# Splitting the operands of a recurrent unit: an early part two units ahead, and token-pair products in 64x64 tiles

## The chip, the cores and the metric

The kernel runs on one core of a Trainium2 chip. A core has a matrix engine (TensorE, in the profile PE, with its weight loads listed apart as PEld), a vector engine (VectorE, DVE), a scalar engine (ScalarE, ACT), a general engine (GpSimd, POOL) and SyncE (SP), which here issues the DMAs. Each engine works through a queue of its own in order and waits on semaphores for the others. Operands lie in SBUF (128 partitions), products of TensorE land in PSUM, and transfers between SBUF and DRAM are DMAs. The metric is the device time of one execution in microseconds (us); less is better.

## The reference, cut to what matters

The program is a decoder trunk of two layers over 1024 tokens of width 1024. Layer 0 mixes tokens by attention, layer 1 by a recurrence (RWKV-7) over 12 heads of 64 channels; both have a feed-forward part. The change is in layer 1's recurrence alone:

```python
def step(S, inp):
    r_t, w_t, k_t, v_t, a_t, b_t = inp
    sa = jnp.einsum("bhij,bhj->bhi", S, a_t)
    S = S * w_t[:, :, None, :] + sa[..., None] * b_t[:, :, None, :] + v_t[..., None] * k_t[:, :, None, :]
    y = jnp.einsum("bhij,bhj->bhi", S, r_t)
    return S, y
```

It is called with `r, decay, k, v, -kk, kk * a`, where `kk` is the normalised key and `a` a gate. Each head has a 64x64 state S, which every token decays, corrects (`sa` by `b`) and adds to (`v` by `k`); `y` reads it out.

## The kernel before, in words

The recurrence is computed in chunks of CH = 64 tokens. Inside a chunk, the tokens' effect on each other is a 64x64 matrix of products of token pairs for each head; the corrections within a chunk need the inverse of a triangular 64x64 matrix made from one of these, called N. Between the chunks the state is carried on, one chunk after the other.

A *unit* n (0 to 11) is four heads (two *pairs*; a pair is two heads on the partition halves A = 0 to 63 and B = 64 to 127) and QT = 256 tokens, thus four chunks. Units 0 to 3 are the four quarters of the tokens of the first two pairs, 4 to 7 of the next two, and so on. The steps of a unit, with their lines:

- `prepare(n)` (from L947): allocates the unit's tiles, loads r, k, v and two gates from DRAM (L964, L967; pool `ld` with two buffers, of which one unit takes two), and normalises the keys (L973 to L992).
- `products(n)` (from L996) calls `unit` for each of two pairs. `unit` (from L1010) makes the running decay with a scan on DVE (L1017), exponentials on ACT (L1020, L1022), the tile AR (the corrected key and r, each decayed) and F, and with the inverse decay BKz, in which each head's rows are written for one head at a time and the other half is zero (L1035, L1037). On PE, BKz against AR in 128x128 tiles gives all token-pair products of one head and chunk (L1042): its rows hold, for one head, N and R in one half and the operands of the sequence in the other. DVE masks them into the tile ARK (L1043); ACT copies N and R out of ARK (L1044, L1045) and then writes AR over their place (L1046). PE transposes BKz (L1052, eight a pair), ACT takes half of it as `bkt` (L1053). `rkk` and `bv` (L1056 to L1059) are for the output. At the end v is transposed into W (L1004 to L1008). ARK has two buffers, used in turn: unit n+2 writes the one that unit n's sequence reads.
- `invert(n)` (from L1063): N goes to DRAM (L1070) and comes back as 16x16 blocks (`nb`, L1072); POOL inverts all blocks at once with 28 small operations that depend on each other (L1077, L1078); the blocks go to DRAM (L1081) and come back as X (L1084). Then two rounds for each pair merge 16x16 blocks to 32x32 and 64x64: a transpose on DVE (L1089), products on PE in 64x64 tiles (L1093, L1099), masking and adding on DVE (L1095, L1100).
- `sequence(n)` (from L1103): for each of four chunks in turn, products of ARK with W (L1124, L1140), a copy Rs (L1134), the product with X (L1146), a copy into W (L1150), the state for the next chunk (L1154, L1157), and the output's part with R (L1116); at the end `yd` is copied out (L1159).
- `finish(n)` (from L1162): normalises the output and stores it.

The order of the program is at L1192 to L1215. In turn n: `sequence(n)`, `invert(n+1)`, `prepare(n+2)`, `finish(n)`, `products(n+2)`. Between them stand *pieces* of other work, 88 in all (`fill`): the input projections of later heads (24 matrix products each, L149 to L151), memory attention, and first parts of the output projection (six matrix products each); 12 run before, seven by FILL[12], and FILL[n] in turn n. They are tied behind the first matmul of each chunk of the turn (`issue_after`). A planner decides each engine's order when the program is built, from its own estimates of time; what is written earlier goes first where both are ready, and on the chip each engine keeps that order. After turn 10, `fill(99)` and the loads for the rest of the output projection are written (L1211 to L1215), ahead of turn 11.

Of the kernel before, what the change touches and what calls it, by code (L numbers as in the profile page):

```python
# [10 lines left out]
F32 = mybir.dt.float32  # L11
# [18 lines left out]
FILL = (4, 4, 3, 4, 5, 3, 11, 9, 8, 9, 9, 0, 7)  # L30
# [36 lines left out]
class Trunk:  # L67
# [588 lines left out]
    def rwkv(self, rows_src):  # L656
# [8 lines left out]
        with ExitStack() as so:  # L665
# [240 lines left out]
            with ExitStack() as s:  # L906
# [33 lines left out]
                for t in XD:  # L940
                    nc.sync.dma_start(t.rearrange("a b -> (a b)").rearrange("(p f) -> p f", p=P), BKz.rearrange("p c h t -> p (c h t)")[:, 0 : PITCH // 16])
# [5 lines left out]
                def prepare(n):  # L947
# [5 lines left out]
                    d["N"], d["R"] = (up.tile([P, 2, NC, CH], F32, name=c) for c in "NR")  # L953
                    d["pC"] = up.tile([P, 2, NC], F32, name="pC", bufs=3)
                    d["bv"] = up.tile([P, 2, QT], F32, name="bv")
                    d["bkt"] = up.tile([P, 2, NC, P], F32, name="bkt")
                    d["W"] = W = up.tile([P, 2, NC, 2, CH], F32, name="W")
                    if q == 0:
                        nc.gpsimd.memset(W[A, :, 0, 0, :], 0.0)
                        nc.gpsimd.memset(W[B, :, 0, 1, :], 0.0)  # L960
# [35 lines left out]
                def products(n):  # L996
                    d = DU[n]
                    ld, W = d["ld"], d["W"]
                    for u in range(2):
                        unit(d, u, ld[u], d["sa"][u], d["kk"][u])  # L1000
# [9 lines left out]
                def unit(d, u, rkv, sga, kk):  # L1010
                    p = d["pa"] + u
                    r, k, v = (rkv[:, j, :] for j in range(3))
                    sg, at = sga[:, 0, :], sga[:, 1, :]
                    ark, Rm, Nm, bkz = d["ark"][:, u], d["R"][:, u], d["N"][:, u], BKz
# [19 lines left out]
                    bz = lambda hd: bkz[:, :, hd, :].rearrange("p c (h t) -> p c h t", h=2)  # L1034
                    nc.vector.tensor_mul(bz(0)[A], F[A], c3(pi)[A][:, :, None, :].broadcast_to([64, NC, 2, CH]))  # L1035
                    for j in range(2):
                        nc.vector.tensor_mul(bz(1)[B, :, j, :], F[B, :, 1 - j, :], c3(pi)[B])  # L1037

                    for R, hd in HD:
                        ga = psg.tile([P, NC, P], F32, name="ps_ga", tag="g")  # L1040
                        for c in range(NC):
                            nc.tensor.matmul(ga[:, c, :], bkz[:, c, hd, :], AR[:, c, :, :].rearrange("p h t -> p (h t)"), start=True, stop=True)  # L1042
                        nc.vector.tensor_mul(ark[:, :, hd, :], ga, MM[:, None, :].broadcast_to([P, NC, P]))  # L1043
                        nc.scalar.copy(Nm[R], ark[R, :, hd, 0:64])  # L1044
                        nc.scalar.copy(Rm[R], ark[R, :, hd, 64:P])  # L1045
                        nc.scalar.copy(ark[R, :, hd, :], AR[R].rearrange("p c h t -> p c (h t)"))  # L1046

                    for c2 in range(0, NC, 2):
                        pbk = psg.tile([P, 2, 4, CH], F32, name="ps_bk", tag="g")
                        for c in range(2):  # L1050
                            for hd in range(2):
                                nc.tensor.transpose(pbk[:, c, 2 * hd : 2 * hd + 2, :], bkz[:, c2 + c, hd, :], self.ident)  # L1052
                        nc.scalar.copy(d["bkt"][:, u, c2 : c2 + 2, :].rearrange("p c (h j) -> p c h j", h=2), pbk[:, :, 0:4:3, :])  # L1053

                    rkk = t1("rkk", tag="sq")
                    nc.vector.scalar_tensor_tensor(c3(rkk), c3(r), self.col("rk", p), F[:, :, 1, :], op0=ALU.mult, op1=ALU.mult)  # L1056
                    pbv = psx.tile([P, QT], F32, name="ps_bv", tag="x")
                    nc.tensor.matmul(pbv, blk, rkk, start=True, stop=True)
                    nc.vector.tensor_mul(d["bv"][:, u, :], pbv, v)  # L1059
# [3 lines left out]
                def invert(n):  # L1063
                    d = DU[n]
                    N = d["N"]
                    nd, xd = ND[n % 2], XD[n % 2]
                    nb = up.tile([64, 16, 16], F32, name="nb", bufs=1)
                    xb = up.tile([64, 16, 16], F32, name="xb", bufs=1)
                    for R, hd in HD:
                        nc.sync.dma_start(rows_of(nd, hd), N[R].rearrange("p u c t -> p (u c t)"))  # L1070
# [9 lines left out]
                    for h in range(8):  # L1080
                        nc.sync.dma_start(blocks_of(xd, h), xb[8 * h : 8 * h + 8])  # L1081
                    d["X"] = X = up.tile([P, 2, NC, CH], F32, name="X")
# [108 lines left out]

                N = 2 * NPAIR  # L1192
                prepare(0)
                products(0)
                invert(0)
                fill(FILL[12])
                prepare(1)
                products(1)
# [704 lines left out]
```

## Time and profile before

| | |
|---|---|
| median of 3 runs | 2689.64 us (2686.9 to 2694.15) |
| profiled execution | 2686.54 us, span 2684.7 us |
| mean granted TensorE clock in it | 0.974 |
| the recurrence's sequences | first ends at 1463.0, last at 1991.8 us |

The page of the profile gives the busy time of each engine; "busy time in stretches" gives, for each stretch of time, its length, then the busy time of PE, PEld, DVE, ACT and POOL with the number of instructions, the TensorE clock that was granted as a share of full speed, the share of DMA time, and GB/s. The timeline has the start, the duration, the engine, the line, and what is written from what; in brackets stands how long the engine sat idle before and what ended it. A row of the waits has the instruction that waited, whom it waited for, the total in us, how often, and the longest. A row of a group has the count, then busy time and mean ns of one, then idle time before it and what ended that. A row that gives "min/median/max" has durations in ns and the first and last start. An fp32 matmul shows as two instructions.

### The profile page before, as it was taken

What the parts mean: (1) busy time and instruction counts of PE and PEld (TensorE: products, weight loads), DVE (VectorE), ACT (ScalarE), POOL (GpSimd) and SP (SyncE); (2) the same over time, 40 slices, a digit from 0 to 9 for tenths busy, and PEclk for the clock granted to TensorE, in tenths of its full rate; (3) what the DMA queues carried; (4) which work ended last, traced back from release to release, by engine and by line L of the source; (5) the groups of instructions that cost most, each with busy time, mean ns of one, the idle gap of its engine ahead of it and who ended that gap; (6) DMA issues with size and microseconds to landing.
All of it is one profiled execution on the core that took longest, in us unless ns stands there. A gap on an engine that the chain in (4) does not pass through costs nothing. (4 is left out here: it accounts for less than half of the span.)

```text
span 2684.7 us, 41293 instructions
## 1 busy us (share of the span) xinstructions
PE 2543.4 (95%) x15901; PEld 2064.7 (77%) x15901; DVE 1795.9 (67%) x3283; ACT 1219.9 (45%) x2032; POOL 222.2 (8%) x525
## 2 busy tenths in 40 slices
PE   8999999999999999999989999889888999999998
PEld 7877776778888788887867777677666888878886
DVE  5567766577666687675246656887669656568677
ACT  4465555254444433348343433564216444443343
POOL 0012232000000000000011211222200000000000
PEclk9999999999999999999999999999889999999999
DMA  4100002334443867535632233324214444386761
GB/s 168 58 26 17 9 21 72 123 108 164 150 147 133 300 247 271 206 106 202 218 107 71 81 99 86 99 74 145 70 57 149 161 153 151 136 332 231 270 228 71
DMA packets 263828, 370.50 MB, mean 138 GB/s; under 512 B 41104, under 2 KB 139792, under 8 KB 263632
## 3 DMA queue, kind: packets, MB, share of 16 engines
q1 hardware_dynamic: 263488, 367.60, 40.1%
q8 instruction: 125, 2.05, 0.3%
q14 instruction: 71, 0.58, 0.1%
q10 hardware_dynamic: 144, 0.26, 0.0%
HBM read 258.75 MB, written 109.05 MB: 137 GB/s over the span
## 5 line engine op out<-in xcount | busy, mean ns | idle before, releaser
L143 ACT CAST Xh<-wraw 128x1024 fp32r<-128x1024 f32 (+1 forms) x138 | 139.8, 1039 | 216.4 <-PE ps_z L1623 75.7
L149 PE MATMUL ps_in<-Xh,whi 128*128 128x512 f32 x480 | 195.8, 410 | 14.5 <-ACT whi L143 8.8
L150 PE MATMUL ps_in<-Xl,whi 128*128 128x512 f32 x480 | 193.1, 402 | 0.5 <-DVE Xl L144 0.5
L151 PE MATMUL ps_in<-Xh,wlo 128*128 128x512 f32 x480 | 193.0, 403 | 0.0
L143 ACT CAST Xl<-wraw 128x1024 fp32r<-128x1024 f32 x103 | 105.2, 1051 | 150.5 <-PE ps_y L1623 48.4
L144 DVE TENSOR_TENSOR Xh<-wraw,Xh 128x1024 fp32r<-128x1024 f32 x115 | 138.0, 1220 | 48.4 <-ACT Xh L143 47.9
L144 DVE TENSOR_TENSOR wlo<-wraw,whi 128x1024 fp32r<-128x1024 f32 (+3 forms) x93 | 105.9, 1139 | 71.5 <-ACT whi L143 70.8
L144 DVE TENSOR_TENSOR Xl<-wraw,Xl 128x1024 fp32r<-128x1024 f32 x103 | 123.8, 1221 | 34.0 <-ACT Xl L143 33.5
L143 ACT CAST whi<-wraw 128x1024 fp32r<-128x1024 f32 (+3 forms) x93 | 88.3, 953 | 120.0 <-PE ps_in L150 51.2
L149 PEld LDWEIGHTS ps_in<-Xh,whi 128*128 128x128 f32 x480 | 92.7, 193 | 36.0 <-ACT whi L143 8.8
L1285 PE MATMUL ps_f<-Xh,N 128*128 128x512 f32 x320 | 106.7, 397 | 4.4 <-ACT N L143 2.7
L151 PEld LDWEIGHTS ps_in<-Xh,wlo 128*128 128x128 f32 x480 | 92.4, 193 | 19.9
L150 PEld LDWEIGHTS ps_in<-Xl,whi 128*128 128x128 f32 x480 | 92.7, 193 | 19.2 <-DVE Xl L144 1.0
L625 ACT ACTIVATE E<-ps_s,mx,SC 128x128 f32<-128x128 f32 (+7 forms) x96 | 79.5, 832 | 51.1 <-DVE mx L623 24.5
L628 POOL TENSOR_TENSOR E<-E,l 128x768 f32<-128x768 f32 (+5 forms) x60 | 83.8, 1401 | 201.6 <-DVE l L626 101.3
L1285 PE MATMUL ps_f<-TB,N 128*128 128x512 f32 x384 | 91.9, 389 | 0.7 <-ACT N L143 0.7
L1623 PE MATMUL ps_y<-Xh 128*128 128x512 f32 x384 | 90.1, 389 | 0.0
L1623 PE MATMUL ps_z<-Xh 128*128 128x512 f32 x384 | 89.6, 389 | 0.0
L1623 PE MATMUL ps_z<-Xl 128*128 128x512 f32 x384 | 89.6, 389 | 0.0
L1623 PE MATMUL ps_y<-Xh,Xh 128*128 128x512 f32 x360 | 85.0, 390 | 0.0
L1285 PEld LDWEIGHTS ps_f<-TB,N 128*128 128x128 f32 x384 | 72.0, 188 | 16.0 <-ACT N L143 1.1
L1623 PEld LDWEIGHTS ps_z<-Xl 128*128 128x128 f32 x384 | 72.1, 188 | 15.0
(519 smaller groups left out, 6611.3 us busy)
## 6 DMA issues: line engine op xcount, KB each, us to landing
wraw<-in_w_ff_dram SPq DMA_DIRECT2D x182, 512.0 KB
wraw<-h_d SPq DMA_DIRECT2D x108, 512.0 KB
h_d<-slot SPq DMA_DIRECT2D x128, 256.0 KB
h_d<-tr SPq DMA_DIRECT2D x64, 256.0 KB
wraw<-in_w_in_dram SPq DMA_DIRECT2D x31, 512.0 KB
lo_d<-l_st SPq DMA_DIRECT2D x36, 256.0 KB
rkv_d<-rkv_st SPq DMA_DIRECT2D x36, 256.0 KB
rkv<-rkv_d SPq DMA_DIRECT2D x24, 384.0 KB
```

The costliest lines, as they stand in the source:

```text
L143: h = self.nc.scalar.copy(hi, src)
L144: l = self.nc.vector.tensor_sub(lo, src, f32(hi))
L149: mm(ps, wh, xh, start=first, stop=False)
L150: mm(ps, wh, xl, start=False, stop=False)
L151: mm(ps, wl, xh, start=False, stop=last)
L625: nc.scalar.activation(E3[:, g, :], S[:, g * w0 : g * w0 + n], AF.Exp, bias=mx[:, g : g + 1], scale=SC[:, i : i + 1], accum_out=l[:, g : g ...
L628: nc.gpsimd.tensor_mul(E3, E3, l[:, :, None].broadcast_to([P, nh, n]))
L1285: yield nc.tensor.matmul(ps, A[x][:, k, :], B[y][:, k, :], start=fresh and k == 0 and i == 0, stop=k == 3 and i == 2, skip_group_check=True)
L1623: m = nc.tensor.matmul(ps[t], A[x][:, u, t * P : (t + 1) * P], B[y][:, u, :], start=fresh and i == u == j == 0, stop=end and i == last_ an ...
```

## The change

- `prepare(n)` no longer allocates N, R, bv, bkt and W. N and R become one tile NR, with three buffers.
- `early(n)` is new: for both pairs `decays` (the first part of the old `unit`: scan, exponentials, AR, F, and BK, now one dense tile without zeros), then the products of each head's own rows with its own columns in 64x64 tiles, masked by DVE straight from PSUM into NR; then `substitute(n)`, the DRAM trips and POOL's chain up to the store of the blocks.
- `late(n)` is new: the other products of token pairs, in 64x64 tiles from the rows of one half to the partitions of the other half, masked into ARK; the copies of AR into ARK; four transposes a pair and not eight; bv, and v into W.
- `merge(n)` is the rest of `invert(n)`, from the load of X on.
- The order in turn n is `sequence(n)`, `merge(n+1)`, `prepare(n+2)`, `early(n+2)`, `finish(n)`, `late(n+2)`. FILL is new, with seven pieces in turn 11, and `fill(99)` with the last loads is written after the last turn.

The core of the diff:

```diff
-FILL = (4, 4, 3, 4, 5, 3, 11, 9, 8, 9, 9, 0, 7)
+FILL = (4, 3, 4, 3, 4, 3, 11, 9, 7, 7, 7, 7, 7)
...
-                BKz = kp.tile([P, NC, 2, P], F32, name="BKz")
-                for t in [cmp_, BKz]:
-                    nc.gpsimd.memset(t, 0.0)
+                nc.gpsimd.memset(cmp_, 0.0)
+                nc.gpsimd.memset(ARK[0], 0.0)
...
-                    d["N"], d["R"] = (up.tile([P, 2, NC, CH], F32, name=c) for c in "NR")
+                    d["NR"] = up.tile([P, 2, NC, 2 * CH], F32, name="NR", bufs=3)
...
+                def early(n):
+                    d = DU[n]
                     for u in range(2):
-                        unit(d, u, ld[u], d["sa"][u], d["kk"][u])
+                        decays(d, u, d["ld"][u], d["sa"][u], d["kk"][u])
+                    substitute(n)
...
+                def late(n):
...
+                    for u in range(2):
+                        ark, AR, BK = d["ark"][:, u], d["AR"][u], d["BK"][u]
+                        ga = psg.tile([P, NC, P], F32, name="ps_ga", tag="g")
+                        for c in range(NC):
+                            for R, hd in HD:
+                                nc.tensor.matmul(ga[HD[1 - hd][0], c, :], BK[R, c, 1, :], AR[R, c, :, :].rearrange("p h t -> p (h t)"), start=True, stop=True)
+                        for R, hd in HD:
+                            O = HD[1 - hd][0]
+                            nc.scalar.copy(ark[R, :, hd, :], AR[R].rearrange("p c h t -> p c (h t)"))
+                            nc.vector.tensor_mul(ark[O, :, hd, :], ga[O], MM[O, None, :].broadcast_to([64, NC, P]))
+
+                        pbk = psg.tile([P, NC, P], F32, name="ps_bk", tag="g")
+                        for c in range(NC):
+                            nc.tensor.transpose(pbk[:, c, :], BK[:, c, :, :].rearrange("p h t -> p (h t)"), self.ident)
+                        nc.scalar.copy(d["bkt"][:, u, :, 0:64], pbk[:, :, 0:64])
+                        for R, hd in HD:
+                            nc.scalar.copy(d["bkt"][R, u, :, 64:P], pbk[HD[1 - hd][0], :, 64:P])
...
-                    AR = tp.tile([P, NC, 2, CH], F32, name="AR")
+                    AR = tp.tile([P, NC, 2, CH], F32, name="AR", bufs=2)
                     F = tp.tile([P, NC, 2, CH], F32, name="F")
+                    BK = tp.tile([P, NC, 2, CH], F32, name="BK", bufs=2)
...
+                    nc.vector.tensor_mul(BK, F, c3(pi)[:, :, None, :].broadcast_to([P, NC, 2, CH]))
+
+                    ga = psg.tile([P, NC, P], F32, name="ps_gn", tag="g")
+                    for c in range(NC):
+                        for R, hd in HD:
+                            nc.tensor.matmul(ga[R, c, :], BK[R, c, 0, :], AR[R, c, :, :].rearrange("p h t -> p (h t)"), start=True, stop=True)
+                    nc.vector.tensor_mul(d["NR"][:, u], ga, MM[:, None, :].broadcast_to([P, NC, P]))
...
+                def substitute(n):
...
+                    N = DU[n]["NR"].rearrange("p u c t -> p (u c) t")[:, :, 0:CH]
...
-                        nc.sync.dma_start(rows_of(nd, hd), N[R].rearrange("p u c t -> p (u c t)"))
+                        nc.sync.dma_start(rows_of(nd, hd).rearrange("s (a t) -> s a t", t=CH), N[R])
...
                 for n in range(N):
                     sequence(n)
                     if n + 1 < N:
-                        invert(n + 1)
+                        merge(n + 1)
                     if n + 2 < N:
                         prepare(n + 2)
+                        early(n + 2)
                     finish(n)
                     if n + 2 < N:
-                        products(n + 2)
+                        late(n + 2)
                     for c, m in enumerate(anchors):
                         with self.tc.issue_after(m):
                             fill((FILL[n] + c) // NC)
-                    if n == N - 2:
-                        fill(99)
-                        self.wo = [self.load_split(a["w_out"][1, k * P : (k + 1) * P, :], (1024,)) for k in (6, 7)]
-                        for kt in (4, 5):
-                            self.fetch_o(kt, kt - 2, slice(0, QT * 3))
+                fill(99)
+                self.wo = [self.load_split(a["w_out"][1, k * P : (k + 1) * P, :], (1024,)) for k in (6, 7)]
+                for kt in (4, 5):
+                    self.fetch_o(kt, kt - 2, slice(0, QT * 3))
```

More of the change, by code (lines that the diff above doesn't have):

```diff
@@ L952, in prepare @@
                     d["ark"] = ARK[n % 2]
-                    d["N"], d["R"] = (up.tile([P, 2, NC, CH], F32, name=c) for c in "NR")
+                    d["NR"] = up.tile([P, 2, NC, 2 * CH], F32, name="NR", bufs=3)
                     d["pC"] = up.tile([P, 2, NC], F32, name="pC", bufs=3)
[L955 to L960, printed above, removed]
+                    d["AR"], d["BK"], d["rkk"] = [], [], []
                     ld, sa = [], []
@@ L994, in prepare @@
                     d["ld"], d["sa"] = ld, sa
[L996 removed]
+                def early(n):
                     d = DU[n]
[L998 removed]
                     for u in range(2):
[L1000 removed]
+                        decays(d, u, d["ld"][u], d["sa"][u], d["kk"][u])
+                    substitute(n)
+                def late(n):
+                    d = DU[n]
+                    ld = d["ld"]
+                    d["bv"] = up.tile([P, 2, QT], F32, name="bv")
+                    d["bkt"] = up.tile([P, 2, NC, P], F32, name="bkt")
+                    d["W"] = W = up.tile([P, 2, NC, 2, CH], F32, name="W")
+                    if n % 4 == 0:
+                        nc.gpsimd.memset(W[A, :, 0, 0, :], 0.0)
+                        nc.gpsimd.memset(W[B, :, 0, 1, :], 0.0)
+                    for u in range(2):
[14 more added lines that the diff above has]
+                            nc.scalar.copy(d["bkt"][R, u, :, 64:P], pbk[HD[1 - hd][0], :, 64:P])
+                        pbv = psx.tile([P, QT], F32, name="ps_bv", tag="x")
+                        nc.tensor.matmul(pbv, blk, d["rkk"][u], start=True, stop=True)
+                        nc.vector.tensor_mul(d["bv"][:, u, :], pbv, ld[u][:, 2, :])
@@ L1008, in products, with decays @@
                         nc.scalar.copy(ev[A, :, :, e, 1, :], pv[R, :, :, 64:P])
-                def unit(d, u, rkv, sga, kk):
+                def decays(d, u, rkv, sga, kk):
                     p = d["pa"] + u
-                    r, k, v = (rkv[:, j, :] for j in range(3))
+                    r, k = rkv[:, 0, :], rkv[:, 1, :]
                     sg, at = sga[:, 0, :], sga[:, 1, :]
-                    ark, Rm, Nm, bkz = d["ark"][:, u], d["R"][:, u], d["N"][:, u], BKz
                     L = t1("L")
@@ L1032, in unit @@
                     nc.vector.tensor_mul(AR[:, :, 1, :], c3(r), pt[:, :, 1:])
[L1034 to L1055, printed above, removed]
@@ L1104, in sequence @@
                     d = DU[n]
-                    ark, Rm, bkt, W, X, pC = (d[k] for k in ("ark", "R", "bkt", "W", "X", "pC"))
+                    ark, bkt, W, X, pC = (d[k] for k in ("ark", "bkt", "W", "X", "pC"))
+                    Rm = d["NR"][:, :, :, CH:]
                     d["yd"] = yd = up.tile([P, 2, NC, CH], F32, name="yd", bufs=1)
@@ L1193, in rwkv @@
                 prepare(0)
-                products(0)
-                invert(0)
+                early(0)
+                late(0)
+                merge(0)
                 fill(FILL[12])
                 prepare(1)
-                products(1)
+                early(1)
+                late(1)
                 for n in range(N):
```

16 lines of the change are left out of this document (9 added, 7 removed).

## The prediction

> **What bounds the kernel now.** I read the page first, then the busy time in stretches, then one unit step by step in the timeline, then the waits.
>
> ```profile
> span 2684.7 us, 41293 instructions
> PE 2543.4 (95%) x15901; PEld 2064.7 (77%) x15901; DVE 1795.9 (67%) x3283; ACT 1219.9 (45%) x2032; POOL 222.2 (8%) x525
> ...
> L1159 ACT COPY yd<-ps_y x12: 584/587/603, 1463.0 to 1991.8; 128x512 f32<-128x512 f32 x12
> ...
> core 0: us, PE busy (x) PEld busy (x) DVE busy (x) ACT busy (x) POOL busy (x), PEclk, DMA share, GB/s
> 1463.00:1992.00 529.00, 473.02 (x5394) 376.44 (x5393) 375.58 (x1071) 222.16 (x510) 103.89 (x342) 0.93 0.30 89
> 1522.00:1563.00 41.00, 38.84 (x434) 31.29 (x435) 24.72 (x70) 16.99 (x34) 11.57 (x37) 1.00 0.28 76
> 1859.00:1922.00 63.00, 52.96 (x613) 41.81 (x611) 43.85 (x116) 17.85 (x39) 13.01 (x32) 0.81 0.24 71
> 1922.00:1955.00 33.00, 31.19 (x352) 23.95 (x348) 22.57 (x63) 9.70 (x23) 8.66 (x30) 1.00 0.16 37
> 1955.00:1992.00 37.00, 25.85 (x351) 21.25 (x349) 21.93 (x58) 7.92 (x11) 0.00 (x0) 0.77 0.20 65
> ```
>
> TensorE bounds the whole (95%), but not evenly. The diff touches only the recurrence, whose twelve sequences end (copy of yd, L1159) between 1463.0 and 1991.8: 528.8 us for eleven units, 48.1 us a unit. There PE is idle for 529 − 473.0 = 56.0 us, and its granted clock averages 0.93, another 0.07 × 529 = 37 us. Busy time at full clock is 473.0 × 0.93 = 440 us. The stretches 1522 to 1563 and 1922 to 1955 show what the filling with other products reaches where nothing waits: 94.6% busy (70.03 of 74) at clock 1.00. The stretches from 1859 and from 1955 are the bad ones. Why, the timeline shows for unit 10 (the times are starts; the second number is the duration):
>
> ```profile
> 1859.42 0.60 ACT L1159 COPY yd<-ps_y 128x512 f32<-128x512 f32 x1
> 1868.02 1.19 SPq L1070 DMA_DIRECT2D nd<-N  x2
> 1868.32 0.40 ACT L1044 COPY N<-ARK 64x256 f32<-64x256 f32 x1
> 1871.41 2.83 SPq L1072 DMA_DIRECT2D nb<-nd  x8
> 1875.64 0.39 POOL L1073 COPY xb<-nb 64x256 f32<-64x256 f32 x1 [10.96 <-DMA nb<-nd]
> 1884.05 0.36 SPq L964 DMA_DIRECT2D rkv<-rkv_d  x1
> 1890.35 0.22 POOL L1078 TENSOR_TENSOR xb<-xb,xtmp 64x14 f32<-64x14 f32 x1
> 1894.90 0.47 SPq L1084 DMA_DIRECT2D X<-xd  x1
> 1898.81 0.45 DVE L1089 STREAM_TRANSPOSE XT<-X 128x256 f32<-128x256 f32 x1 [6.79 <-DMA X<-xd]
> 1918.59 0.40 ACT L1044 COPY N<-ARK 64x256 f32<-64x256 f32 x1 [0.49 <-DVE ARK L1043]
> 1923.46 0.42 DVE L1100 TENSOR_TENSOR X<-X,ps_x 128x256 f32<-128x256 f32 x1
> 1954.73 0.59 ACT L1159 COPY yd<-ps_y 128x512 f32<-128x512 f32 x1 [15.86 <-PE ps_y L1116]
> ```
>
> Sequence 8 ends at 1859.4. Unit 10 writes the same one of two ARK buffers, and N is copied out of ARK, so its products finish only then: N is there at 1868.7, 9.3 us later. Two trips through DRAM and the chain on POOL (1875.6 to 1890.6) follow; X is first used at 1898.8, 30.1 us after N. The merging ends at 1923.9 (25.1 us), sequence 10 at 1954.7 (30.8 us). That is a loop of 95.3 us over two units, 47.7 us a unit, and the measured mean is 48.1: this loop sets the pace, and PE is filled or not filled inside it.
>
> **The change part by part.** *The loop.* N now comes out of PSUM straight into NR (three buffers), needs no ARK, and its substitution is written right behind it. What ties unit n+2 back is its rkv tile (two sets, last read by late(n+1), which follows the end of sequence n−1). So the new loop runs over three units. Its terms by the stretched values of the same unit: late 9.3 (as the products from 1859.4), loading rkv to N 34.9 (1884.05 to 1918.99, unit 11), N to X 30.1, merging 25.1, sequence 30.8: 130.2 us, 43.4 us a unit. Against it stands PE: 440 us of work at the 94.6% of the good stretches is 465 us, 42.3 us a unit. The larger, 43.4, sets the pace: 11 × (48.1 − 43.4) = −52 us. DVE would be busy for 375.6/11 = 34.1 us of each unit, 79%: third, not first. The waits that go are those for X (first row: what DVE's transposes L1089 waited for, in all and how often), and those of PE, in whose queue the merging (L1099) stands ahead of the sequence:
>
> ```profile
>   DMA X<-xd: 22.0, 8
> ...
> SPq L1070 <- ACT R L1045: 126.4, 20, 33.5
> ...
> PE ps_x L1099 <- DVE Q L1095: 12.1, 10, 3.2
> PE ps_y L1140 <- DVE W L1157: 11.1, 20, 2.3
> ```
>
> DVE sat idle 22.0 us for X, eight times. What is late next is in the last row, the sequence's own short steps; they stay. On SP the store of N waited 126.4 us; it waits still, now for NR, with the loads of nb, rkv and weights queued behind it. I price that at nothing since it comes a sequence earlier; if the cover fails, one longest wait (33.5) is lost.
>
> *PE.* Only these rows show the sizes concerned:
>
> ```profile
> 1926.64 1.95 PE L1042 MATMUL ps_ga<-AR,BKz 128*128 128x128 f32 x16
> 1928.51 0.45 PE L1146 MATMUL ps_q<-Rs,X 64*64 64x64 f32 x8
> 1928.89 0.50 PE L149 MATMUL ps_o<-whi,Xh 128*128 128x512 f32 x1
> ...
> 1958.10 0.63 PE L1093 MATMUL ps_q<-XT,N 64*64 64x64 f32 x16
> ...
> L1093 PE MATMUL ps_q<-XT,N x768: 218/218/366, 1411.1 to 1966.2; 64*64 64x64 f32 x192
> ...
> L1052 PE MATMUL ps_bk<-cst,BKz 128*128 128x128 f32 x192 | 28.4, 280 | 2.0 <-ACT bkt L1053 0.9 <-DVE ARK L1043 0.7
> ```
>
> Products: 16 instructions a pair, each 0.28 us long (the mean of L1052, of the same shape), so a new one every (1.95 − 0.28)/15 = 0.11 us: 1.8 us. After: 32 of 64x64 with 128 columns. L1093's 64x64, 64 columns, start every (0.63 − 0.22)/15 = 0.027 us, so two run side by side, and 128 columns should take 0.055 each: 1.8 us, no difference. Half of them now cross (rows A to columns B), which no row shows; if those do not run side by side, 16 × 0.055 × 24 pairs = +21 us of PE. Could they be cheaper? The arithmetic is the same, so I see no end below nothing and take 0, as L1093 is the nearest row. Transposes: 8 to 4 a pair, 96 × 0.11 = −10.6 us.
>
> Against this stands the switch between tile shapes. The last L1042 starts at 1926.64 + 15 × 0.11 = 1928.3, the burst of 64x64 0.2 later and not 0.11; its 8 take 8 × 0.027 = 0.22, and the next starts after 0.38. A burst so costs 0.09 + 0.16 = 0.25 us beyond its work. Two new bursts a pair, 48 in all: +12 us. Together +1 us. [...]
>
> *DVE and ACT.*
>
> ```profile
> L1043 DVE TENSOR_TENSOR ARK<-ps_ga,cm 128x512 f32<-128x512 f32 x48 | 32.4, 683 | 12.1 <-PE ps_ga L1042 12.0
> L1037 DVE TENSOR_TENSOR BKz<-F,pi 64x256 f32<-64x256 f32 x48 | 19.4, 422 | 1.0
> L1017 DVE TENSOR_TENSOR_SCAN L<-rm,sga 128x256 f32<-128x256 f32 x24 | 16.4, 683 | 7.5 <-DMA sga<-lo_d 6.9 <-ACT pt L1020 0.5
> L1035 DVE TENSOR_TENSOR BKz<-F,pi 64x512 f32<-64x512 f32 x24 | 16.1, 671 | 1.0 <-PE ps_bk L1052 0.9
> L1044 ACT COPY N<-ARK 64x256 f32<-64x256 f32 x48 | 19.4, 404 | 45.0 <-DVE ARK L1043 44.5
> L1053 ACT COPY bkt<-ps_bk 128x256 f32<-128x256 f32 x48 | 16.7, 371 | 8.0 <-PE ps_bk L1052 4.7 <-PE ps_q L1154 2.8
> ```
>
> DVE a pair: out 2 × 0.68 + 0.67 + 2 × 0.42 = 2.9; in one BK and three maskings, 0.67 + 3 × 0.68 = 2.7: −4 us over 24 pairs, behind PE, priced at 0. ACT: out two N and two R copies of one shape, 4 × 0.40, and 2 × 0.37 = 2.3, in three copies at 0.37 = 1.1; −30 us, but ACT is busy 222 of 529: it shortens only the start, where nothing is ahead. There N of unit 0 loses, in each of two pairs, a masking and two N copies, 1.5 us: −3 us. N now leaves in runs of 256 bytes, not 2 KB; nb comes in runs of 64 and is used 1.4 us after its last issue (1874.24 to 1875.64), so between 0 and some 2 us more, off the path by a sequence: 0. The larger memset stands ahead of the first load, with nothing behind it: 0. On PE the early products wait for BK with sequence n's steps queued behind; in the kernel before they wait for BKz in front of sequence n+1's: 0, and beyond that it is rival B.
>
> *Pieces and the end.* The 88 pieces of other work stay, the last seven move behind sequence 11, which had none: this lets the poor last stretch (1955 to 1992) reach the pace above. But the last loads move too:
>
> ```profile
> 1956.10 1.99 ACT L143 CAST whi<-wraw 128x1024 fp32r<-128x1024 f32 x2 [0.78 <-PE ps_o L151]
> 1973.16 0.81 SPq L348 DMA_DIRECT2D wraw<-o_d  x2
> 1989.26 1.23 DVE L144 TENSOR_TENSOR slot<-wraw,slot 128x1024 fp32r<-128x1024 f32 x1
> ```
>
> The casts of w_out 6 and 7 start as soon as the last piece frees their buffers (1956.1); fetching and the other weights end at 1990.5, all beside sequence 11. After the change the casts follow a piece pinned to sequence 11, and some of the 17.3 us from 1973.16 to 1990.5 stands bare: between 0 and 17; I take 6, since products with the first two weights, and finishing unit 11, still cover most.
>
> Sum: −52 + 1 − 3 + 6 = −48 us. The profiled execution took 2686.5 (span 2684.7 and 1.8 around it), 3.1 below the median 2689.6. So 2638.5 for its like, 2641.6 for the median: 2642.
>
> **The rivals.** *A, PE was the bound all along.* For it: the pieces are conserved, and most waits for X pass while PE works on pieces. Against: 93 us of idle time and clock. Left are the start and the end, −3 + 6, and small waits: 2680 to 2693. *B, slower: DVE's queue.* The early part (scan 0.68, five products of 256 elements at the 0.42 of L1037, BK 0.67, masking 0.68: 4.1 us a pair, 8.3 a unit) now stands among the steps of sequence n; every step waits for a short DVE copy. In the kernel before the same work stands beside sequence n+1 in part, so at most half is new: 4.1 × 11 = +45 us, 2735. It decides if the sequence's chain, not PE or the loop, sets the pace, that is if sequences take above 43 us each. Against: DVE is 71% busy, and sequences took 31 us. *C, the change does not do what it says*: rkv and the preparing, not ARK, hold N back, since they too wait their turn on PE and DVE. Then the 34.9 us term grows by the 9.3 that it no longer shares, 139.5/3 = 46.5: −18 us + 4, 2676.
>
> **How the numbers follow.** Forecast 0.62, A 0.14, B 0.14, C 0.10. The forecast's own spread: the loop can shrink to PE's 42.3 and the start improve, and since PE's busy time counts the tail of every small burst, 42.3 is no hard floor: DVE's 34.1 is the next, half way to it is 38.2, and 11 × (48.1 − 38.2) = 109 less 4 gives 2585 at the far end, 2595 with most of it; upward +21 for crossing tiles, +11 at the end. The range 2595 to 2690 takes in C and most of A and leaves out B and the far end. A measurement here can tell about 0.3%, 8 us, from no change. Faster: 0.62 + 0.09 (C) + 0.04 (A) = 0.75; same 0.10 (A) + 0.01 (C) = 0.11; slower 0.14 (B).
>
> **What would show it.** Right: yd copies some 43 us apart; N stored before the sequence two units back ends; DVE's wait for X near zero; PEclk near 1.00 from the tenth unit on; 96 transposes fewer; L1042's successor in twice as many 64x64 instructions. Wrong: yd still 48 apart with N early (A); Rs and W copies waiting behind the scan and BK, sequences above 43 us (B); N stored as late as now (C); a gap of over 10 us before the first output rows.

## The result: slower by 1.2%

The changed kernel took 2720.61 us (median of 4 runs, 2719.09 to 2722.41), the kernel before 2688.27 us (2685.24 to 2694.15) beside it: ratio 1.0118, 95% interval 1.0099 to 1.0137. The forecast was 2642 and the range ended at 2690. The profiled execution of the changed kernel took 2722.41 us.

From the page of the changed kernel, then the group of its copies of yd (durations, then first and last start), then the busy time in stretches for the recurrence and for units 1 to 3 one by one (columns as in the prediction: length, busy time of PE, PEld, DVE, ACT and POOL, clock, DMA share, GB/s):

```profile
span 2720.6 us, 41742 instructions
PE 2552.2 (94%) x16189; PEld 2064.3 (76%) x16189; DVE 1795.9 (66%) x3259; ACT 1194.1 (44%) x1960; POOL 212.1 (8%) x525
...
L1177 ACT COPY yd<-ps_y x12: 562/585/594, 1459.7 to 2013.9; 128x512 f32<-128x512 f32 x12
...
1460.00:2014.00 554.00, 473.38 (x5594) 372.36 (x5592) 370.43 (x1049) 197.59 (x449) 92.63 (x341) 0.90 0.28 83
...
1460.00:1518.00 58.00, 48.86 (x585) 39.45 (x585) 37.26 (x106) 19.89 (x43) 9.94 (x38) 0.85 0.25 73
1518.00:1566.00 48.00, 46.89 (x520) 36.69 (x514) 30.31 (x88) 16.76 (x34) 9.85 (x36) 1.00 0.31 90
1566.00:1622.00 56.00, 46.39 (x498) 36.87 (x494) 32.21 (x92) 17.32 (x38) 9.11 (x38) 0.85 0.28 78
```

The span grew by 35.9 us, and the copies of yd split it in three. Up to the first one the kernel gained 3.3 us (1463.0 to 1459.7). From the first to the last it lost 25.4 (528.8 to 554.2, 50.4 us a unit where 43.4 was forecast). Behind the last it lost 13.8 (692.9 to 706.7). In the recurrence PE was busy as long as before (473.4 against 473.0 us), so the 25 us are idle time: 80.6 us where it had been 56.0. The granted clock fell as well, from 0.93 to 0.90, so the same busy time did less work: 473.4 × 0.90 = 426 us at full clock instead of 440, with 96 transposes fewer (11 us by the prediction's price). The units from 1460 and from 1566 have clock 0.85, the one between them 1.00.

Was N early? In the timeline, unit 9 (start, duration, engine, line, what; in brackets the idle time before it and what ended that):

```profile
1810.12 0.36 SPq L958 DMA_DIRECT2D rkv<-rkv_d  x1
...
1818.70 2.86 SPq L1093 DMA_DIRECT2D xd<-xb  x8
1822.26 1.44 SPq L958 DMA_DIRECT2D rkv<-rkv_d  x1
1826.78 0.51 ACT L967 ACTIVATE sq<-rkv,vec 128x256 f32<-128x256 f32 x1 [3.30 <-DMA rkv<-rkv_d]
...
1835.49 0.59 ACT L1177 COPY yd<-ps_y 128x512 f32<-128x512 f32 x1
1841.92 0.87 DVE L986 SCALAR_TENSOR_TENSOR kk<-rkv,vec,ps_kb 128x256 f32<-128x256 f32 x2
1853.19 1.22 SPq L1082 DMA_DIRECT2D nd<-NR  x2
1861.32 0.36 SPq L958 DMA_DIRECT2D rkv<-rkv_d  x1
1862.29 0.37 ACT L1034 COPY W<-ps_vt 64x256 f32<-64x256 f32 x1
```

Sequence 7 ends at 1835.5, and N of unit 9 is stored at 1853.2, 17.7 us later. Over units 2 to 11 it came 1 to 24 us after the end of the sequence two units back (mean 14.9); in the kernel before, 8 to 33 us (mean 19.0). The rows show what holds it. The first load of rkv starts at 1810.1, the second, behind the eight stores of xd, which wait 8.1 us for POOL, at 1822.3; the keys are normalised at 1841.9, N is stored 11.3 us later, v goes into W 9.1 us after that, and the buffers are free as soon as v has been read for it: the next unit's rkv is loaded at 1861.3. This is a loop of 51.2 us over *one* unit. It is not a fixed length: with the same tile, e2 below needs 47.2 us a unit.

The waits in 1470 to 1940 show it as idle time (what waited for what, total in us, times, longest), and below stands what DVE's transposes of X waited for:

```profile
ACT sq L967 <- DMA rkv<-rkv_d: 56.3, 13, 10.3
...
DVE F L1058 <- DMA rkv<-rkv_d: 40.5, 8, 9.8
...
  DMA X<-xd: 35.6, 10
```

ACT and DVE sat idle for rkv, and DVE waited for X, which was to be there early, longer than before (22.0 us).

The sequence's own wait for X is another matter. In its first chunk a sequence copies Rs and then needs X for its next product. Unit 1 in the kernel before, then the busy time while it waited for X:

```profile
1467.83 0.28 DVE L1134 COPY Rs<-ps_q 128x128 f32<-128x128 f32 x1
1479.94 0.33 PE L1146 MATMUL ps_q<-Rs,X 64*64 64x64 f32 x4
1519.04 0.59 ACT L1159 COPY yd<-ps_y 128x512 f32<-128x512 f32 x1 [1.98 <-PE ps_y L1116]
...
1468.10:1479.90 11.80, 11.80 (x160) 9.90 (x158) 9.06 (x30) 7.25 (x17) 0.14 (x2) 1.00 0.12 25
```

and in the changed kernel, then the busy time of the rest of its sequence:

```profile
1464.15 0.28 DVE L1152 COPY Rs<-ps_q 128x128 f32<-128x128 f32 x1
1465.49 0.33 PE L1164 MATMUL ps_q<-Rs,X 64*64 64x64 f32 x4 [1.00 <-DVE X L1117]
1518.09 0.56 ACT L1177 COPY yd<-ps_y 128x512 f32<-128x512 f32 x1
...
1465.60:1518.00 52.40, 44.61 (x490) 35.82 (x492) 31.98 (x93) 17.74 (x39) 9.84 (x37) 0.84 0.26 75
```

Cut in this way, units 1 to 11 took in the mean (in brackets PE's idle time in all eleven; yd is that of the sequence before, then the unit's own):

| | yd to the end of Rs | Rs to the first product with X | from there to yd |
|---|---|---|---|
| before | 4.4 us (0.9) | 10.4 us (12.9) | 33.3 us (42.1) |
| changed | 5.2 us (5.2) | 4.5 us (5.7) | 40.7 us (69.7) |

So the wait for X did shrink, by 5.9 us a unit, and the rest of the sequence grew by 7.4. In the kernel before, PE worked on pieces and other products for all but 12.9 of the 114 us of that wait. Most of its idle time lay behind it, among the sequence's other steps, and there it grew.

### The profile page after: what moved, and what is told of

It is laid out like the page before. It is cut to its first block, busy times and chain, and to the rows that moved or that the text cites. A ratio compares the mean times of both kernels' runs of the same rounds, so it can differ in the third digit from the quotient of the medians.

```text
span 2720.6 us, 41742 instructions
## 1 busy us (share of the span) xinstructions
PE 2552.2 (94%) x16189; PEld 2064.3 (76%) x16189; DVE 1795.9 (66%) x3259; ACT 1194.1 (44%) x1960; POOL 212.1 (8%) x525
## 5 line engine op out<-in xcount | busy, mean ns | idle before, releaser
L1643 PEld LDWEIGHTS ps_y<-Xh 128*128 128x128 f32 x384 | 72.1, 188 | 15.0
```

Source lines behind the costliest of these rows:

```text
L1643: m = nc.tensor.matmul(ps[t], A[x][:, u, t * P : (t + 1) * P], B[y][:, u, :], start=fresh and i == u == j == 0, stop=end and i == last_ an ...
```

## The experiments

Three theories stood after the result. Theory 1: the tile of r, k and v, free only when the late part of the unit before has read v, makes each unit wait for the one before. Theory 2: the early part stands in the queues of PE and DVE among the sequence's steps (rival B). Theory 3: the new counts of pieces and the later place of the last loads, and not the recurrent unit's own steps. Times of a whole kernel are medians, stretches inside it are from its profiled execution; each ratio is to the kernel before on the same chip, with its 95% interval.

**e1, v apart.** The changed kernel, with v in a tile of its own.

```diff
-t = lp.tile([P, 3, QT], F32, name="rkv")
+t = lp.tile([P, 2, QT], F32, name="rk")
+tv = lp.tile([P, QT], F32, name="vv", bufs=4)
```

> The changed kernel, with v loaded into a tile of its own (four buffers); r and k keep two buffers, which are free once the early part of the unit before has read them. Theory 1 (the rkv tile is held until late(n+1), so that loading, preparing, early and late of one unit after the other form a loop of about 50 us, which sets the pace of the changed kernel): N is stored some 9 to 10 us earlier in each unit, the yd copies stand about 44 us apart and not 50.4, so 40 to 70 us less than the changed kernel, about 2660. Theory 2 (the pace is set by the queues of PE and DVE, whose order puts the early part among the sequence's steps): no change, within 10 us of 2720, and the yd copies still 50 apart. Theory 3 (the loss is in the pieces and the end): no change in the recurrence.

Measured: 2681.54 us, ratio 0.9979 (0.9968 to 0.999), 45.7 us a unit where 44 was expected. The recurrence takes 502.9 us and no longer 554.2, so the tile does cost time. The way to it was not the expected one: N of unit 2 is stored 35 us earlier, but in units 3 to 11 it still comes 12.4 us behind the sequence two units back, where it was 14.9. A unit's wait for X stays as it was (4.1 us for 4.5), and the rest of its sequence falls from 40.7 to 37.1 us.

**e2, the pieces as before.** The changed kernel with the old FILL, and `fill(99)` and the last loads after turn 10.

```diff
-FILL = (4, 3, 4, 3, 4, 3, 11, 9, 7, 7, 7, 7, 7)
+FILL = (4, 4, 3, 4, 5, 3, 11, 9, 8, 9, 9, 0, 7)
...
+if n == N - 2:
+    fill(99)
```

> The changed kernel with the FILL of the kernel before, and the last loads again behind turn 10. Theory 3 (pieces and the end: last sequence to the end of the span takes 706.7 us after the change, 692.9 before): the end comes back to about 693, so 14 us less, about 2707, and if the distribution of pieces is also what slows the recurrence, down to 2690. Theory 1 (the loop of loading, preparing, early and late): the recurrence from the first to the last yd copy stays at about 554 us or gets longer, since the last sequence again has no pieces; total 2707 to 2720.

Measured: 2674.89, ratio 0.9955 (0.9939 to 0.9972): 46 us less than the changed kernel, more than either theory expected. By the two profiled executions, 51 us apart, 35 lie in the recurrence (47.2 us a unit) and 15 behind it.

**e3, the tiles alone.** e2 with the order of before; `early` no longer ends with `substitute`.

```diff
+substitute(n + 1)
 merge(n + 1)
 if n + 2 < N:
     prepare(n + 2)
-    early(n + 2)
 finish(n)
 if n + 2 < N:
+    early(n + 2)
     late(n + 2)
```

> The 64x64 tiles alone: NR, BK and the new products, but in the order of the kernel before (early and late of a unit written together behind finish, the substitution together with the merging, the old FILL and the old place of the last loads). If the tiles cost nothing, as the pairs of 64x64 instructions 0.109 us apart say: within 10 us of the kernel before, 2680 to 2698. If switching tile shapes and the third masking on DVE are what slows the changed kernel: about 2720. Theory 1 has no view of the sign, but expects N as late as before.

Measured: 2678.63, ratio 0.9974 (0.996 to 0.9988). The 64x64 tiles, with NR and the dense BK, bring about 7 us; the split on top of them (e2) 4 more, which the intervals don't tell apart. In the two traces PE's instructions stand in the same order from the first yd up to 1804 us, but for one place: the planner had already put the early steps where they are ready, so writing them earlier moves almost nothing.

**e4, v apart with the pieces of before.** The edits (and diffs) of e1 and e2 together.

> Both: v apart, and FILL and last loads as before. Theory 1 with theory 3 for the end: as v apart, 2660, and another 14 us less for the end, but with a last sequence that has no pieces: 2640 to 2665. Theory 2: 2707.

Measured: 2667.67, ratio 0.9932 (0.9915 to 0.9949), 45.4 us a unit.

Either edit alone takes the loss back, so pieces and tile cause it together. The recurrence in us:

| | new pieces | pieces of before |
|---|---|---|
| v in one tile with r and k | 554.2 (changed) | 519.2 (e2) |
| v apart | 502.9 (e1) | 499.3 (e4) |

The new pieces cost 35 us beside the shared tile and 3.6 without it; the shared tile costs 51 us with the new pieces and 20 with the old. The next four take theory 3 apart.

**e5, before with the new pieces.** The opposite of e2's edit, on the kernel before.

```diff
-FILL = (4, 4, 3, 4, 5, 3, 11, 9, 8, 9, 9, 0, 7)
+FILL = (4, 3, 4, 3, 4, 3, 11, 9, 7, 7, 7, 7, 7)
```

> The kernel before with the changed kernel's counts of pieces and its place of the last loads, and nothing else of the change. If these two cost by themselves, as taking them back saved 46 us, the kernel before grows by 20 to 46 us, to 2707 to 2733, with a bare gap before the first output rows. If they cost only where the split makes each unit serial, it stays within 8 us of 2688, or pays the end alone (about 14 us: 2702). If the order of the pieces is a matter of chance, anything from 2670 to 2720 may come, and the place in time of the loss differs from that in the changed kernel.

Measured: 2695.22, ratio 1.0033 (1.0018 to 1.0048), 9 us. By its trace they lie at the end alone: the recurrence takes 525.1 us where it was 528.8, the time behind it 706 where it was 693. The new counts by themselves do not slow the recurrence of the kernel before.

**e6, early counts as before.** The changed kernel, last loads at the end.

```diff
-FILL = (4, 3, 4, 3, 4, 3, 11, 9, 7, 7, 7, 7, 7)
+FILL = (4, 4, 3, 4, 5, 3, 11, 9, 7, 7, 7, 5, 7)
```

> The changed kernel with the counts of before in turns 0 to 4 only (4,4,3,4,5 for 4,3,4,3,4; five in turn 11), the last loads still behind the last turn. If the early counts made the recurrence slow, it takes back most of the 35 us of the recurrence (yd to yd 520 us, total about 2685). If the late counts or the place of the loads did, it stays at 545 to 555 us and about 2715. By chance of the order: between.

Measured: 2683.78, ratio 0.9987 (0.9971 to 1.0003), 47.0 us a unit. Turns 0 to 4 carry 37 of the 46 us.

**e7, the last loads back.** The changed kernel with its FILL; `fill(99)` and the last loads after turn 10.

```diff
+if n == N - 2:
+    fill(99)
```

> The changed kernel with its own counts of pieces, but the rest of the pieces and the last loads written after turn 10, as before. If the place of the loads costs at the end alone, the tail falls from 707 to about 692 us and the recurrence stays at 554: about 2706. If the pieces behind the last turn also slow the recurrence, the recurrence falls by some 35 us too: about 2675.

Measured: 2716.28, ratio 1.0111 (1.0086 to 1.0136), the recurrence 551.7 us, the time behind it 702.3. The place alone is worth 4 us, no more than a measurement can tell.

**e8, a neutral move.** e2 with one piece moved from turn 3 to turn 2.

```diff
-FILL = (4, 4, 3, 4, 5, 3, 11, 9, 8, 9, 9, 0, 7)
+FILL = (4, 4, 4, 3, 5, 3, 11, 9, 8, 9, 9, 0, 7)
```

> The changed kernel with the pieces and last loads of before, and one piece moved from turn 3 to turn 2, which should cost nothing by any theory of mine: 2675, within 5 us, if times follow from the counts and the loops. If the planner's order makes times a matter of chance, it may move by 10 to 40 us from the 2674.9 of its twin.

Measured: 2670.8, ratio 0.9938 (0.9918 to 0.9959); e2's interval overlaps. A shuffle of the pieces is not a matter of 40 us here. But its recurrence is 14 us shorter than e2's and the time behind it 14 us longer, so the parts of a run are known less well than their sum.

**e9, before with v apart** (the diff of e1, on the kernel before), and **e10, e4 without the split** (the diff of e3, on e4).

> The kernel before with v loaded into a tile of its own (four buffers), r and k in another (two). In before, N needs ARK, which the sequence two units back frees, so an earlier load of r and k should bring nothing: 2680 to 2694. If the shared tile of r, k and v is a bound of its own there too (rival C of the prediction), it gains as the changed kernel does: 7 us or more, 2680 or less.

> The kernel with v apart and the pieces of before (2667.7), but with the order of before: the whole of the preparing behind finish, the substitution with the merging. Only the 64x64 tiles, NR and the separate v stay. If the split in two parts brings something once v is apart, this is slower than its twin by 8 us or more (2676 or more) and N is stored later. If the planner makes nearly the same order of both, as it did without v apart (2674.9 against 2678.6, the first eight units within 2 us of each other), it is within 8 us of it.

Measured: e9 2673.86, ratio 0.9954 (0.9936 to 0.9972); e10 2671.82, ratio 0.9954 (0.9936 to 0.9972). The shared tile held the kernel before back too, by 13 us. The split is worth some 4 us beside e4, too little to tell from none.

**e11, four pieces a turn,** and **e12, three buffers,** both on e4.

```diff
-FILL = (4, 4, 3, 4, 5, 3, 11, 9, 8, 9, 9, 0, 7)
+FILL = (4, 4, 4, 4, 4, 3, 11, 9, 8, 9, 9, 0, 7)   # e11
-AR = tp.tile([P, NC, 2, CH], F32, name="AR", bufs=2)
+AR = tp.tile([P, NC, 2, CH], F32, name="AR", bufs=3)   # e12, and BK, rkk
```

> v apart, the last loads after turn 10, and four pieces in each of turns 0 to 4, so that the first chunk of each of these turns has a piece. If a turn without a piece in its first chunk leaves TensorE idle and its clock halved there, the first units gain: below 2667.7, some 2655 to 2665, and the clock in units 1 to 5 is 0.97 or more. If only the sum of the early pieces matters, it is within 5 us of 2667.7.

> v apart and the pieces of before, with three buffers instead of two for AR, BK and rkk, which also tie the early part of a unit to the late part of the one before. If these buffers are the next bound, N is stored earlier again and the recurrence falls below 499 us, total 2650 to 2662. If the order of the short steps in the queues bounds it now, no change: 2667.7 within 5 us.

Measured: e11 2662.01, ratio 0.9907 (0.9884 to 0.993); e12 2663.78, ratio 0.992 (0.9899 to 0.994). Both intervals overlap e4's, and the recurrence took 498.6 and 499.2 us against 499.3: neither is the next bound. In e11 the clock is 1.00 in units 1 to 4, as expected, and 0.88 in unit 5; no time in the recurrence came of it.

**e13, where the turn's hole is.** The changed kernel with its own counts; the extra pieces of a turn go to its first chunks and no longer to its last, so in a turn of three another chunk goes without one.

```diff
-fill((FILL[n] + c) // NC)
+fill((FILL[n] + NC - 1 - c) // NC)
```

> The changed kernel with its own counts of pieces, only spread the other way over the four chunks of a turn: three pieces now go to the first three chunks, and the last goes without. If the empty first chunk costs (PE without pieces from 1458 to 1481 us in the changed kernel, clock 0.85 in unit 1), it takes back most of the 35 us of the recurrence: about 2685. If the number of the early pieces decides, it stays at 2710 to 2722.

Measured: 2689.63, ratio 1.0005 (0.9995 to 1.0014): this one expression takes back 31 us. The stretches in which a turn of three pieces begins, in the changed kernel (turns 1, 3 and 5):

```profile
1458.00:1482.00 24.00, 19.23 (x286) 15.43 (x285) 20.80 (x57) 10.45 (x24) 0.92 (x5) 0.86 0.21 59
1566.00:1590.00 24.00, 19.27 (x264) 15.81 (x260) 21.23 (x55) 10.23 (x24) 2.79 (x13) 0.86 0.31 89
1681.00:1700.00 19.00, 15.56 (x244) 13.05 (x244) 17.29 (x48) 9.29 (x21) 0.21 (x2) 0.82 0.23 61
```

and in e13:

```profile
1458.00:1482.00 24.00, 21.75 (x308) 17.37 (x308) 20.49 (x55) 13.12 (x28) 0.88 (x6) 0.93 0.28 81
1559.00:1583.00 24.00, 23.53 (x308) 18.97 (x305) 17.28 (x45) 9.35 (x20) 9.81 (x32) 1.00 0.28 78
1648.00:1668.00 20.00, 18.22 (x284) 14.60 (x278) 17.90 (x51) 8.74 (x22) 0.21 (x2) 1.00 0.27 82
```

With the same number of pieces, PE is busy 91 to 98% of these stretches and no longer 80 to 82%, and the clock is 0.93 to 1.00 and no longer 0.82 to 0.86. DVE is busy 17 to 21 us of each in both: its work with the new unit and the sequence's small steps sits there, and in the first stretch of the changed kernel 4.7 of PE's 4.8 idle us end with DVE. A piece fills such a gap. By whole units, turns 1 and 3 gain 11 and 12 us and turn 4, whose pieces stand as they did, 13; turn 5 loses 3. The spells of half clock in the trace add up to 109.2 us in the recurrence of the changed kernel, 54.6 in e13, 71.7 in the kernel before, 58.0 in e5. Why the same bare chunks cost nothing in e5 and 3.6 us with v apart (e1) stays open.

**e14, another bank for bv.** In e4, N still came 7 us behind the sequence two units back in the mean of ten units, and 17 in unit 4 (below: yd at 1547.15, N stored at 1563.83). The next tie shows in its timeline:

```profile
1536.70 0.59 PE L1028 MATMUL ps_bv<-rkk,cm 128*128 128x256 f32 x2
1538.07 0.61 PE L972 MATMUL ps_ss<-hsel,sq 128*128 128x2 f32 x4
1541.45 0.61 PE L972 MATMUL ps_ss<-hsel,sq 128*128 128x2 f32 x4
1547.15 0.58 ACT L1179 COPY yd<-ps_y 128x512 f32<-128x512 f32 x1 [7.56 <-PE ps_y L1136]
...
1554.33 0.83 DVE L988 SCALAR_TENSOR_TENSOR kk<-rk,vec,ps_kb 128x256 f32<-128x256 f32 x2
1563.83 1.28 SPq L1084 DMA_DIRECT2D nd<-NR  x2
```

The product for the key's norm (ps_ss) of unit 4 starts right behind the one for bv of unit 3, the last step of that unit's late part: both use the only buffer of the pool `psx`. The edit, on e4:

```diff
-pbv = psx.tile([P, QT], F32, name="ps_bv", tag="x")
+pbv = psg.tile([P, QT], F32, name="ps_bv", tag="g")
```

> v apart, pieces of before, and the product for bv in the bank of the token-pair products and not in the one of the key's norm. If the shared bank ties the preparing of a unit to the end of the late part of the one before (ps_ss started 1.4 us after ps_bv), the keys are normalised earlier, N is stored before the sequence two units back ends, and the recurrence falls below 499 us: 2650 to 2662. If the queues' order bounds it: 2667.7 within 5 us.

Measured: 2644.45, ratio 0.9843 (0.9825 to 0.9861), 23 us less than e4. Its timeline, a unit later (yd is that of unit 3, kk and N are unit 5's), and its copies of yd and its recurrence as a whole:

```profile
1574.72 0.61 PE L972 MATMUL ps_ss<-hsel,sq 128*128 128x2 f32 x4 [0.34 <-ACT o L1207]
1576.55 0.70 PE L1028 MATMUL ps_bv<-rkk,cm 128*128 128x256 f32 x2
...
1589.70 0.87 DVE L988 SCALAR_TENSOR_TENSOR kk<-rk,vec,ps_kb 128x256 f32<-128x256 f32 x2
...
1601.17 1.22 SPq L1084 DMA_DIRECT2D nd<-NR  x2
1604.11 0.59 ACT L1179 COPY yd<-ps_y 128x512 f32<-128x512 f32 x1 [0.19 <-PE ps_y L1136]
```

```profile
L1179 ACT COPY yd<-ps_y x12: 572/586/589, 1458.0 to 1940.4; 128x512 f32<-128x512 f32 x12
...
1458.00:1940.00 482.00, 439.70 (x5509) 344.91 (x5507) 366.66 (x1029) 196.47 (x442) 89.45 (x313) 0.97 0.32 97
```

The key's norm now starts ahead of bv, N is stored 2.9 us before the sequence two units back ends (over all ten units 17 us before to 20 behind, mean 3 behind), and a unit takes 43.9 us. The wait for X is nearly that of e4 (4.6 us a unit for 5.1), the rest of the sequence takes 33.1 us for 34.7, PE's idle time falls from 54.0 to 42.7 us and the spells of half clock from 44.0 to 24.6. So the other bank gains, but that it does so by the earlier N is not shown.

**e15, all together** (e14 with the diffs of e11 and e12), and **e16, e15 without the split** (the diff of e3).

> v apart, four pieces in each of turns 0 to 4, last loads after turn 10, three buffers for AR, BK and rkk, and bv in the other bank. The gains of e11 and e12 over e4 were 6 and 4 us; with the bank's own 5 to 15 us: 2645 to 2660. If these ties are one and the same slack, no better than e11: 2662.

> e15 with the order of before: early part and substitution behind finish and with the merging. If the split pays once nothing ties it, this is slower than e15 by 8 us or more. If the planner's order makes the place in the program immaterial, within 8 us of e15.

Measured: e15 2674.04, ratio 0.9949 (0.9934 to 0.9964); e16 2673.37, ratio 0.9952 (0.9935 to 0.9969). A miss: two edits, each harmless on e4, cost 30 us on e14. Which of them does it was not tried. N comes earlier there than in e14 (1 us behind in the mean in e15, level in e16), so an early N alone does not make the time.

**e17, e14 without the split** (the diff of e3), and **e18, e14 with one piece moved** (the diff of e8).

> e14 without the split: early part and substitution back to their places of before, all else as in e14. If the split pays now that N is stored about when the sequence two units back ends, this is slower by 8 us or more: 2652 or more. If the planner makes the same of both orders, as in e3 and e10, 2640 to 2650.

> e14 with one piece moved from turn 3 to turn 2. If the bank is worth the 23 us, 2636 to 2653, as the same move cost or gained 4 us in e8. If e14 is a lucky order, it goes back towards e4: 2655 to 2675.

Measured: e17 2659.33, ratio 0.9911 (0.9888 to 0.9933); e18 2641.74, ratio 0.9846 (0.9816 to 0.9876). The bank's gain stays when a piece is moved. The split is worth 15 us here, and nothing in e15 and e16. It doesn't come from an earlier N: in e17, N is stored 17 us before to 19 behind the sequence two units back, mean 2. What it comes from stays open. e14 and e18 are the fastest found, about 1.5% below the kernel before and 2.8% below the changed one (2644.45 against 2720.61).

## Why the prediction was wrong

**What failed: the loop, and the sequence in it.** The words "this loop sets the pace" put the 48.1 us a unit down to the wait for N and X, and the sequence behind it stood in the sum with "sequence 30.8" and "the sequence's own short steps; they stay". The wait went as the change meant it to: 10.4 to 4.5 us a unit, 65 us in all. It could buy little, since PE had been idle for only 12.9 us of it, and the sequence did not stay: from its first product with X it took 40.7 us instead of 33.3, 82 us more in all, with 69.7 us of PE idle in it instead of 42.1.

**The tie.** "What ties unit n+2 back is its rkv tile (two sets, last read by late(n+1), which follows the end of sequence n−1). So the new loop runs over three units." The tie was seen, and only followed in the direction of the sequence. There are two buffers, but a unit takes both, so it is one set. From late(n+1) the tie goes on: rkv of n+2, its preparing, its late part, rkv of n+3. That loop closes over one unit, 51.2 us in the rows above, and is longer than the 43.4 of the three-unit loop. In the recurrence the tile costs 51 us with the new pieces and 20 with the old. The term of −52 us fell to what e2 and e3 show: the split brings some 4 us while the tile is shared, too little to tell from none. That N would follow two trips and POOL's chain unhindered was wrong for SP's queue as well: the second load of rkv stood 12.1 us (1810.12 to 1822.26) behind stores that waited for POOL, where the store of N and the loads behind it had been priced at nothing.

**The kernel before was read from one good unit.** The 9.3 us from the end of a sequence to N were unit 10's. Over ten units it was 8 to 33, mean 19.0. An N that only waited for ARK would always have come after the same 9 us; that it didn't was the sign that something else held it too. The shared tile is one part: v apart gained 13 us there (e9). But N still came 16.4 us behind in e9's mean, so the rest of its delay stays open. The sequence of unit 10 was a short one as well, 26.2 us from its first product with X to yd, where the eleven units have 22.9 to 44.3. The loop over ARK, 47.7 us a unit against a measured 48.1, agreed by accident of the unit.

**What turned the sign: the pieces,** which had no price but at the end ("The 88 pieces of other work stay, the last seven move behind sequence 11"). A turn of three instead of four leaves its first chunk without one, since (3 + 0) // 4 is 0; the new FILL has this in turns 1, 3 and 5, the old one in turns 2 and 5. e6 puts 37 us on the early counts and e13 31 of them on the chunk, both beside the shared tile; with v apart the new pieces cost the recurrence 3.6 us, and in the kernel before none. It took the pieces, the shared tile and the new steps together, and no rival named it. "PEclk near 1.00 from the tenth unit on" did come true (0.90 in unit 9, then 1.00 and 1.00 in the stretches from 1944 and 1985, where it had been 1.00 and 0.77), and so did the better last stretch: it was paid for in turns 1 to 5.

**The end** was mis-sized within its bounds: +13.8 for a forecast 6, of 0 to 17. What was named as a danger is there, a wait before the output rows:

```profile
2023.99 1.22 PE L149 MATMUL ps_o<-slot,Xh 128*128 128x512 f32 x2 [6.85 <-ACT slot L143]
```

The five kernels with the last loads at the end took 706 to 708 us behind the last yd, the fifteen others of this study 692 to 705, mean 699, so the place is worth some 8 us on average, and 4 in e7. Since e2 and e8, which differ in one piece, are 692 and 705, this is rough.

**What held.** The start: −3 forecast, −3.3 measured; in e2, e6, e7, e8 and e13, whose steps up to there are the same, the first yd lies between 1456.3 and 1462.8 us, so the close agreement may be luck. ACT: −30 forecast, 222.2 to 197.6 us in the recurrence. PE's prices: 

```profile
L1020 PE MATMUL ps_bk<-cst,BK x96: 271/273/478, 1375.2 to 1949.9; 128*128 128x128 f32 x96
...
1520.62 1.09 PE L1066 MATMUL ps_gn<-AR,BK 64*64 64x128 f32 x16
1522.26 1.09 PE L1012 MATMUL ps_ga<-AR,BK 64*64 64x128 f32 x16
```

Sixteen instructions on a head's own rows and sixteen that cross take 1.09 us each, (1.09 − 0.27)/15 = 0.055 us apart, as worked out; the +21 us for crossing fall away, and the transposes are half. That the tile switch costs 0.25 us a burst was not measured by itself; that the tiles as a whole gain 7 us (e3) speaks against a cost beyond the 12 us in the sum.

**The rivals.** C named the mechanism, "rkv and the preparing, not ARK, hold N back", and its time of 2676 is that of e2 (2674.9), the change without the new pieces; but N came only 4 us earlier than in the kernel before (14.9 us behind for 19.0), and the sequence's wait for X fell all the same, so its time agrees by luck. B's sign, sequences above 43 us, shows in units 1, 3, 4 and 5 (49 to 53 us from the first product with X), and DVE is why PE ran dry in the chunks without a piece. As the only cause B falls, since v apart took 51 us off the recurrence (e1) with the same work in DVE's queue. A's reason was right, "most waits for X pass while PE works on pieces". That PE was the bound all along is not: e14 does the recurrence in 482 us with the same pieces and products. The forecast pace of 43.4 us a unit was reached in e14 and e18 (43.9 and 43.7), with v apart, bv in another bank and the old pieces. That this is the three-unit loop is not shown: PE is busy 439.7 of 482 us there, and e17 is slower with N as early.

## What to carry to other kernels

When a step is to move earlier, follow every buffer that it needs to its last reader, and that reader's own inputs on, until the loop closes: the shortest loop in units, and not the longest chain, may be the bound, and one shared tile or one PSUM buffer can be enough for it. Take a term of a loop from all units, and let its spread tell whether the reason holds. Before a wait is priced, look at what the busiest engine did meanwhile: a wait that it fills with other work is worth nothing. Filler work is part of the schedule: an integer division decided which stretches had none, and beside the shared tile that cost 31 us, more than the split ever brought here. Two causes can need each other, so try them in all four combinations.

## What the runs showed of the hardware

TensorE's clock was halved where the longest pause in the 3.4 us before was 1.00 us. In the recurrence of the changed kernel the trace's clock record has 17 spells of half clock, of 3.41, 6.83, 10.24 or 13.65 us. Stretches of 3.4 us, the shortest spell, one after the other:

```profile
1459.20:1462.60 3.40, 3.40 (x71) 3.02 (x70) 2.86 (x8) 1.26 (x3) 0.37 (x2) 1.00 0.03 9
1462.60:1466.00 3.40, 2.05 (x52) 1.60 (x48) 3.40 (x10) 1.66 (x4) 0.10 (x1) 1.00 0.20 75
1466.00:1469.40 3.40, 2.99 (x36) 2.61 (x34) 3.40 (x12) 2.71 (x6) 0.10 (x1) 0.50 0.23 77
1469.40:1472.80 3.40, 2.54 (x40) 2.01 (x40) 3.29 (x12) 1.05 (x4) 0.00 (x0) 0.99 0.27 77
1472.80:1476.20 3.40, 1.62 (x36) 1.38 (x36) 3.15 (x10) 1.10 (x3) 0.00 (x0) 1.00 0.29 76
1476.20:1479.60 3.40, 3.03 (x28) 2.37 (x22) 2.95 (x6) 1.02 (x2) 0.00 (x0) 0.51 0.17 18
...
1465.49 0.33 PE L1164 MATMUL ps_q<-Rs,X 64*64 64x64 f32 x4 [1.00 <-DVE X L1117]
```

PE busy 2.05 of 3.40 us, and the next stretch has half the clock; 2.54 of 3.40, and the next has the whole; 1.62, and half again. In the first of these the longest pause is the 1.00 us of the last row, and the pauses add up to 1.35 us, 40% of the stretch. The sixteen instructions of L1066 took 1.97 us from 1467.01, at half clock, and 1.09 us from 1470.09, at full clock. Over the recurrence of the changed kernel, cut into such stretches from the trace's clock record, 17 of 129 at full clock were followed by half clock: those had PE busy for 6 to 60%, and of the others all but two (57 and 60%) for more than 60. In the kernel before, two with 65 and 73% were followed by half clock too, so the line is not sharp.
